# W_G of blocks 0 and 1 a block later, between W_A and W_B, by seven half-size products in turn, with its normalized rows kept in DRAM

## The chip, the cores and the metric

One Trainium2 chip; the program runs on one of its cores. The metric is the device time of one execution in microseconds, lower is better. A core has a matrix engine (PE, with its weight loads shown as PEld), a vector engine (DVE), a scalar engine (ACT), GpSimd (POOL), a synchronisation engine (SP), and 16 DMA engines that all queues share. In this kernel weights are asked for on SP's queue (q1 in the profile) and activations mostly on POOL's (q0).

## What is computed

One encoder layer over 2048 prompt tokens and 64 sample tokens, all matrices 1024 wide, fp32. Cut to what matters here:

```python
h = rms_norm(x, g_pre)
vA, bA, cA, zA, q, f, iv, zB, gA, gB = split_cols(h @ w_in)
yA = (silu(zA) * bA * causal_conv3(cA * vA)) @ w_a_out             # W_A
yB = (o * silu(zB)) @ w_b_out                                      # W_B, o from the HGRN2 scan
merged = sigmoid(gA) * yA + sigmoid(gB) * yB
x = x + rms_norm(merged @ w_o, g_post)                             # W_O
gate = sigmoid(rms_norm(x, g_ple) @ w_ple_gate)                    # W_G
x = x + (p @ w_ple_proj) * gate
```

The last two lines are the subject: `h2 = rms_norm(x, g_ple)` is multiplied by the gate matrix W_G, and the output is `x + p*gate`, where `p` stands here for the projected `p @ w_ple_proj`.

## The kernel before

The 2112 tokens are three blocks of 704 columns (BN), each two halves of 352 (HN). Activations are feature-major: eight tiles of 128 x 704, one for each 128 features, in a ring of 52 tiles (tag `r`), plus nine half-wide ones (`hf`). Every fp32 product is three matmuls: weights and activations are split into a rounded high part and a low rest (`split`: one ACT copy, one DVE subtraction), and hi*hi, hi*lo and lo*hi are added up in PSUM (five banks `pg` for these products). A matmul takes one 128 x 128 weight and 352 columns.

A weight tile is 128 x 512 fp32, 256 KB: half of one 128-wide column of a matrix. `load_raw` asks SP for it (five buffers `raw`), ACT makes `hi` (four buffers), and the low part is either made by DVE or, when it was stored in DRAM earlier (`lows`), loaded by SP into one of seven buffers (`lo`, four, and `s`, three).

Large products go three ways:

- plain (`gemm`, lines 530 to 539): 16 weight tiles and 384 matmuls for a 1024 x 1024 matrix and one block. Each weight tile (with its low part) serves 24 matmuls.
- Strassen-Winograd by column pair (`sgroup`, lines 343 to 386): seven products of half size in place of eight, all seven at once.
- the same seven products in turn (`in_turn`, lines 464 to 517): product n = 0 to 6 over all four column pairs g, then the next n. 336 matmuls for a matrix and block; each weight tile serves 12 matmuls, since each of the seven products has its own combined weight (`A11, A12, S2, S3, A22, S1, S4`; the S tiles are sums made once and stored in DRAM, by `prepare_sums`, lines 303 to 341). The activations' combinations are made by DVE and ACT one product ahead (`operand_of`, lines 452 to 462, called by `prepare`). After product 1, 4, 5 and 6 of a pair a `sink` takes a finished half tile. A generator yields after each product, and the caller then issues the loads for what follows.

The order of a block: attention path (`path_b`), convolution path (`path_a`), W_A, W_B (together `merge` in block 0, in turn in blocks 1 and 2), W_O (in turn in block 2 only, else plain, `final_out`), then seven groups of the next block's gates (`run(fills, LEAD)`, line 1381), under which `final_norm` makes the new `x` and `h2` a step at a time, then W_G (`final_gate`, line 1383), and the next block's path_b. In blocks 0 and 1, `final_norm` spills `x` to DRAM, splits `h2` into hi and lo tiles, and `final_gate` does eight plain `gemm`s, reloads `x` and `p`, applies the sigmoid and stores `y_fm`. The third block's W_G is done at the end of the program, half by half.

Queues are served in order: a DMA that POOL issues waits for its operand, and those behind it wait too. Reloads marked `pace=True` wait for the last matmul traced so far (line 242). Instructions within an engine stand in the order that the tile scheduler gave them at build time, and ring tiles are handed out in the order of the program.

The sums of W_A and W_B are prepared in block 0 under `merge`; those of W_O under block 1's `path_a`, one column pair for each of its last four steps j (`side`, lines 1331 to 1337).

Of the kernel before, what the change touches and what calls it, by code (L numbers as in the profile page):

```python
# [82 lines left out]
def hybrid_step(  # L83
# [219 lines left out]
    def prepare_sums(firsts, ahead):  # L303
# [23 lines left out]
        for n, (i1, _) in enumerate(groups):  # L327
            a11, a21, a22, a12 = nxt
            if ahead and n + 1 < len(groups):
                nxt = load(*groups[n + 1])  # L330
            V.tensor_tensor(a22, a21, a22, ALU.add)
            keep("S1", i1, a22)
            V.tensor_tensor(a21, a11, a21, ALU.subtract)
            keep("S3", i1, a21)
            V.tensor_tensor(a11, a22, a11, ALU.subtract)
            keep("S2", i1, a11)
            V.tensor_tensor(a12, a12, a11, ALU.subtract)
            keep("S4", i1, a12)
            if not ahead and n + 1 < len(groups):
                nxt = load(*groups[n + 1])  # L340
            yield
# [740 lines left out]
    def merge_in_turn(a, kept, mg, made):  # L1082
# [31 lines left out]
        ], loads  # L1114

# [25 lines left out]
    def final_norm(bl, segs, xo, acc, h2, kept):  # L1141
# [26 lines left out]
        for j in range(KB):  # L1168
            xj = xo[j][:, c]
            if kept is not None:  # L1170
                kept["x", j] = spill("x", j)
                G.dma_start(kept["x", j], xo[j])
            if len(h2) <= j:
# [6 lines left out]
    def final_gate(bl, segs, xo, h2, kept, anew=False):  # L1180
        c = slice(segs[0]["off"], segs[-1]["off"] + HN)
        for j in range(KB):
            if not bl["last"]:
                pss = gemm(W_G + j, h2, segs)
            elif j == 0:
# [4 lines left out]
            xj = reload(kept["x", j]) if ("x", j) in kept else xo[j]  # L1190
            pj = kept["p", j] if bl["last"] else reload(kept["p", j])
# [5 lines left out]
            (SP if bl["last"] and j >= KB - 2 else G).dma_start(y_fm[j * P : (j + 1) * P, segs[0]["t0"] : segs[0]["t0"] + len(segs) * HN], t[:, c])  # L1197
# [122 lines left out]
    for bi, bl in enumerate(blocks):  # L1320
# [8 lines left out]
        sums_ahead = prepare_sums((W_A, W_B), True) if first else prepare_sums((W_O,), False) if bi == 1 else iter(())  # L1329
# [19 lines left out]
        else:  # L1349
# [22 lines left out]
        if nxt:  # L1372
# [10 lines left out]
            run(final_gate(bl, segs, xo, h2, kept))  # L1383
        else:
            gate = [final_gate(bl, [s], xo, h2, kept, anew=s is segs[1]) for s in segs]
# [54 lines left out]
```

## Time and profile before

| | |
|---|---|
| device time, median of 3 runs | 2664.5 us (2657.28, 2667.55, 2664.5) |
| span of the profiled execution | 2661.4 us, 3.1 us under that median; its page gives no time outside the span |
| busy: PE, PEld, DVE, ACT, POOL | 99%, 98%, 65%, 54%, 13% of the span |
| moved by DMA | 735.00 MB, mean 276 GB/s |
| W_G of block 0, of block 1 | 969.4 to 1031.0 us, 1825.1 to 1886.8 us |
| W_A and W_B in turn, block 1 | 1545 to 1655 us |
| W_A, W_B, W_O in turn, block 2 | 2400 to 2565 us |

The matrix engine hardly ever waits. A matmul of 352 columns is shown as some 324 ns long, but matmuls overlap, so that the distance from one to the next, about 160 ns, is what counts: a stretch's length divided by its matmuls. In the windows view each row gives a stretch, its length, the busy time and (in brackets) the number of instructions of each engine, the granted PE clock, the share of time that the 16 DMA engines were busy, and GB/s.

### The profile page before, as it was taken

How to read it: one execution, taken by the hardware profiler on the slowest of the kernel's cores; microseconds unless marked ns; L12 is line 12 of the kernel's file. 1: busy time of each engine (PE TensorE's matmuls, PEld its weight loads, DVE VectorE, ACT ScalarE, POOL GpSimd, SP SyncE). 2: the span in 40 equal slices, each digit the busy share in tenths (PEclk: the TensorE clock that was granted, in tenths of full speed). 3: DMA queues.
4: the chain of work that ended last, by engine and by line, in shares of the span. 5: the costliest groups of instructions: out<-in, count | busy, mean ns of one | idle time of the engine just before them, and what ended most of it. 6: DMA issues, size and time to landing. Idle time of an engine off the chain costs nothing.

```text
span 2661.4 us, 47775 instructions
## 1 busy us (share of the span) xinstructions
PE 2623.0 (99%) x16748; PEld 2600.4 (98%) x16748; DVE 1727.0 (65%) x3341; ACT 1449.6 (54%) x2782; POOL 349.1 (13%) x649
## 2 busy tenths in 40 slices
PE   7999999999999999999999999999999999999998
PEld 7999999999999999999999999999999999999988
DVE  7788888998667545466645578443355564447857
ACT  5655655454334544566645565454566654445664
POOL 1000000100432210001112210021000000001011
PEclk9999999999999999999999999999999999999999
DMA  8677777898998988776789988599867678889975
GB/s 304 217 263 269 244 260 271 299 316 288 367 344 285 352 289 275 252 227 221 222 287 357 391 304 306 182 352 307 276 218 222 222 224 263 273 274 319 302 234 168
DMA packets 362097, 735.00 MB, mean 276 GB/s; under 512 B 44064, under 2 KB 48704, under 8 KB 361856
## 3 DMA queue, kind: packets, MB, share of 16 engines
q1 hardware_dynamic: 324864, 588.20, 65.9%
q0 software_dynamic: 36704, 143.70, 14.9%
q8 instruction: 132, 2.16, 0.3%
q14 instruction: 109, 0.89, 0.1%
q10 hardware_dynamic: 288, 0.05, 0.0%
HBM read 525.71 MB, written 206.06 MB: 275 GB/s over the span
## 4 chain that ended last, share of the span: by engine, by line
PE 88%; DMA 4%; issue 3%; DVE 3%; ACT 1%; POOL 1%; SPq 0%; DVEq 0%; ACTq 0%; POOLq 0%
PE pg L357 19%; PE pg L358 19%; PE pg L359 19%; PE pg L523 4%; PE pg L525 4%; PE pg L524 4%; PE pg L491 3%; PE pg L490 3%; PE pg L492 3%; PE pa L957 1%; PE pa L921 1%; PE pa L911 1%; PE pa L959 1%; PE pa L910 1%; DMA low<-s 1%
## 5 line engine op out<-in xcount | busy, mean ns | idle before, releaser
L357 PE MATMUL pg<-r,hi 128*128 128x352 f32 x3304 | 1095.0, 332 | 6.8 <-DVE r L403 2.7
L358 PE MATMUL pg<-r,hi 128*128 128x352 f32 x3304 | 1070.1, 324 | 0.0
L359 PE MATMUL pg<-r,lo 128*128 128x352 f32 x2356 | 763.6, 324 | 0.0
L214 ACT CAST hi<-raw 128x512 fp32r<-128x512 f32 x708 | 435.6, 619 | 573.1 <-PE pg L358 206.5
L357 PEld LDWEIGHTS pg<-r,hi 128*128 128x128 f32 x3304 | 624.3, 189 | 12.6 <-DVE r L865 4.6
L358 PEld LDWEIGHTS pg<-r,hi 128*128 128x128 f32 x3304 | 623.9, 189 | 0.0
L359 PEld LDWEIGHTS pg<-r,lo 128*128 128x128 f32 x2356 | 443.9, 188 | 0.0
L359 PE MATMUL pg<-r,s 128*128 128x352 f32 x948 | 306.9, 324 | 0.0
L523 PE MATMUL pg<-r,hi 128*128 128x352 f32 x896 | 289.4, 325 | 3.1 <-ACT r L1194 2.1
L524 PE MATMUL pg<-r,hi 128*128 128x352 f32 x896 | 289.8, 324 | 0.6 <-DVE r L184 0.6
L525 PE MATMUL pg<-r,lo 128*128 128x352 f32 x756 | 244.6, 324 | 0.4 <-DVE lo L184 0.2
L184 ACT CAST hi<-raw 128x512 fp32r<-128x512 f32 x234 | 143.4, 619 | 165.4 <-PE pg L358 48.3
L184 DVE TENSOR_TENSOR r<-r,r 128x352 fp32r<-128x352 f32 (+3 forms) x274 | 169.9, 638 | 60.7 <-ACT r L184 60.0
L184 DVE TENSOR_TENSOR lo<-raw,hi 128x512 fp32r<-128x512 f32 x234 | 159.6, 688 | 65.8 <-ACT hi L184 54.2
L184 ACT CAST r<-r 128x352 fp32r<-128x352 f32 (+3 forms) x274 | 150.4, 578 | 75.1 <-DVE r L666 18.2
L184 ACT CAST hi<-s 128x512 fp32r<-128x512 f32 x160 | 99.1, 619 | 154.8 <-PE pg L358 132.7
L491 PE MATMUL pg<-r,hi 128*128 128x352 f32 x560 | 181.8, 326 | 0.0
L359 PEld LDWEIGHTS pg<-r,s 128*128 128x128 f32 x948 | 178.9, 189 | 0.1
L490 PE MATMUL pg<-r,hi 128*128 128x352 f32 x560 | 178.4, 326 | 0.1
L523 PEld LDWEIGHTS pg<-r,hi 128*128 128x128 f32 x896 | 168.0, 188 | 5.5 <-ACT r L1194 2.4
L524 PEld LDWEIGHTS pg<-r,hi 128*128 128x128 f32 x896 | 168.6, 188 | 2.0 <-DVE r L184 1.7
L371 ACT COPY hf<-pg 128x352 f32<-128x352 f32 x354 | 156.0, 446 | 6.9 <-PE pg L359 6.3
(358 smaller groups left out, 4096.9 us busy)
## 6 DMA issues: line engine op xcount, KB each, us to landing
raw<-w_blk SPq DMA_DIRECT2D x590, 256.0 KB, 4.0
lo<-low SPq DMA_DIRECT2D x404, 256.0 KB, 3.9
raw<-S SPq DMA_DIRECT2D x392, 256.0 KB, 4.1
low<-lo SPq DMA_DIRECT2D x346, 256.0 KB, 3.8
s<-low SPq DMA_DIRECT2D x304, 256.0 KB, 3.9
S<-s SPq DMA_DIRECT2D x160, 256.0 KB, 3.3
r<-w_blk POOLq DMA_DIRECT2D x48, 256.0 KB, 7.3
S<-r POOLq DMA_DIRECT2D x48, 256.0 KB, 6.1
```

Source lines behind the costliest of these rows:

```text
L184: return A.copy(hi, src).ins, V.tensor_tensor(lo, src, hi.bitcast(F32), ALU.subtract).ins
L214: A.copy(hi, raw)
L357: add(hi[:, k, :], xhi, start=start and k == 0, stop=False)
L358: add(hi[:, k, :], xlo, start=False, stop=False)
L359: last[0] = add(lo[:, k, :], xhi, start=False, stop=k == KH - 1).ins
L371: copied = A.copy(got[n], ps[bank])
L490: add(hi[:, k, :], xhi, start=start and k == 0, stop=False)
L491: add(hi[:, k, :], xlo, start=False, stop=False)
L492: last[0] = add(lo[:, k, :], xhi, start=False, stop=k == KH - 1).ins
L523: T.matmul(ps, hi[:, k % 4, :], xhi[:, c], start=k == ks[0], stop=False)
L524: T.matmul(ps, hi[:, k % 4, :], xlo[:, c], start=False, stop=False)
L525: last[0] = T.matmul(ps, lo[:, k % 4, :], xhi[:, c], start=False, stop=k == ks[-1]).ins
```

## The change

W_G of block b (b = 0, 1) is no longer done at the end of block b. Its `h2` rows, not split, are written to DRAM by `final_norm`. In block b + 1 a new stage stands between W_A and W_B in the list that `in_turn` works through: seven products in turn on W_G, with `h2`, `x` and `p` loaded from DRAM on POOL's queue, and a sink that applies the sigmoid and stores `y_fm` in half tiles. The loads of the `o` rows and of the first `GB` gates, which W_B needs, move from W_A's products 3, 5 and 6 to W_G's. For the seven products W_G needs sums: `prepare_sums` makes them under block 1's `path_a`, with the low parts of three plain tiles for each pair as well, and W_O's sums move to block 2's `path_a`. The third block's W_G stays plain at the end; it takes stored low parts where there are any, and splits the other tiles anew.

```diff
-                parts.append(split_w(raw, None if anew else (idx, half_)))
+                parts.append(split_w(raw, None if anew or (idx >= W_G and (idx, half_) not in lows) else (idx, half_)))
...
-    def prepare_sums(firsts, ahead):
+    def prepare_sums(firsts, ahead, plain=False):
...
             a11, a21, a22, a12 = nxt
+            for t, key in ((a11, (i1, 0)), (a12, (i1, 1)), (a22, (i1 + KH, 1))) if plain else ():
+                lows[key] = dram.tile([P, 4, P], F32, tag=f"lo{key}", name=nm("low"), bufs=1)
+                lo = tile_of(F32R)
+                split(t, lo, lo)
+                G.dma_start(lows[key], lo.bitcast(F32))
...
-                (W_A, 3): ("o", ob),
-                (W_A, 5): ("o", ob),
-                (W_A, 6): (GB, mg),
+                (W_G, 3): ("o", ob),
+                (W_G, 5): ("o", ob),
+                (W_G, 6): (GB, mg),
                 (W_B, 1): (GB, mg),
...
+    def gate_in_turn(bl, kept):
+        h2, xp = [], {}
+        def fetch(j, h, pair):
+            for kind, t in zip("xp", pair):
+                G.dma_start(t, kept[kind, j][:, h * HN : (h + 1) * HN])
+            xp[j, h] = pair
+        def loads(idx, n):
+            if (idx, n) in ((W_A, 3), (W_A, 5)):
+                h2.extend(reload(kept["h2", j], True) for j in range(len(h2), len(h2) + KH))
+            if (idx, n) in ((W_A, 6), (W_G, 4)):
+                for j in range(0, KH, 2):
+                    both = rt(), rt()
+                    for q in range(2):
+                        fetch(j + q, int(idx == W_G), [half(t, q) for t in both])
+            if (idx, n) == (W_G, 1):
+                for j in range(KH, KB):
+                    both = rt(), rt()
+                    for h in range(2):
+                        fetch(j, h, [half(t, h) for t in both])
+        def sink(g, c, h, x, y):
+            j = g + c * KH
+            v = whole(x, y)
+            gate = hf() if y is None else v
+            A.activation(gate, v, AF.Sigmoid)
+            xt, pt = xp.pop((j, h))
+            V.tensor_tensor(pt, pt, gate, ALU.mult)
+            V.tensor_tensor(pt, pt, xt, ALU.add)
+            o = bl["t0"] + h * HN
+            G.dma_start(y_fm[j * P : (j + 1) * P, o : o + HN], pt)
+        return dict(idx=W_G, raw=h2, sink=sink, anew=()), loads
...
             V.scalar_tensor_tensor(t[:, c], xj, g_ple[:, j : j + 1], rs2[:, c], ALU.mult, ALU.mult)
-            split(t[:, c], h2[j][0][:, c], h2[j][1][:, c])
+            if kept is not None:
+                kept["h2", j] = spill("h2", j)
+                G.dma_start(kept["h2", j], t)
+            else:
+                split(t[:, c], h2[j][0][:, c], h2[j][1][:, c])
...
-        sums_ahead = prepare_sums((W_A, W_B), True) if first else prepare_sums((W_O,), False) if bi == 1 else iter(())
+        sums_ahead = prepare_sums((W_A, W_B), True) if first else prepare_sums((W_G,) if bi == 1 else (W_O,), False, bi == 1)
...
             stages, loads = merge_in_turn(a, kept, mg, made)
+            gate, gate_loads = gate_in_turn(blocks[bi - 1], kepts[bi - 1])
+            stages.insert(1, gate)
...
             for idx, n in in_turn(stages, a_first):
                 loads(idx, n)
+                gate_loads(idx, n)
...
-            run(final_gate(bl, segs, xo, h2, kept))
```

More of the change, by code (lines that the diff above doesn't have):

```diff
@@ L1176, in final_norm, with final_gate @@
             V.scalar_tensor_tensor(t[:, c], xj, g_ple[:, j : j + 1], rs2[:, c], ALU.mult, ALU.mult)
[L1177 removed]
+            if kept is not None:
[3 more added lines that the diff above has]
+                split(t[:, c], h2[j][0][:, c], h2[j][1][:, c])
             yield
[L1180 removed]
+    def final_gate(bl, segs, xo, h2, kept, anew):
         c = slice(segs[0]["off"], segs[-1]["off"] + HN)
         for j in range(KB):
[L1183 to L1185 removed]
+            if j == 0:
                 both = gemm_by_k([W_G, W_G + 1], h2, segs, anew)
@@ L1189, in final_gate @@
                 pss = both[1] if j == 1 else gemm(W_G + j, h2, segs, anew)
-            xj = reload(kept["x", j]) if ("x", j) in kept else xo[j]
-            pj = kept["p", j] if bl["last"] else reload(kept["p", j])
+            xj, pj = xo[j], kept["p", j]
             t = rt()
@@ L1196, in final_gate @@
             V.tensor_tensor(t[:, c], t[:, c], xj[:, c], ALU.add)
-            (SP if bl["last"] and j >= KB - 2 else G).dma_start(y_fm[j * P : (j + 1) * P, segs[0]["t0"] : segs[0]["t0"] + len(segs) * HN], t[:, c])
+            (SP if j >= KB - 2 else G).dma_start(y_fm[j * P : (j + 1) * P, segs[0]["t0"] : segs[0]["t0"] + len(segs) * HN], t[:, c])
             yield
@@ L1382, in hybrid_step @@
             assert not hooks
-            run(final_gate(bl, segs, xo, h2, kept))
         else:
-            gate = [final_gate(bl, [s], xo, h2, kept, anew=s is segs[1]) for s in segs]
+            gate = [final_gate(bl, [s], xo, h2, kept, s is segs[1]) for s in segs]
             spread_out((norms[0], (2, 1, 0, 0, 1, 1, 4, 4)), (norms[1], (0,) * 6 + (1, 1) + (2, 2, 2, 2, 1, 0, 1, 3, 3, 2)))
```

2 lines of the change are left out of this document (1 added, 1 removed).

## The prediction

> **What bounds the kernel now.** I read the page's head first, then the stretches of the stages that the change touches, then the DMA issues.
>
> ```profile
> span 2661.4 us, 47775 instructions
> PE 2623.0 (99%) x16748; PEld 2600.4 (98%) x16748; DVE 1727.0 (65%) x3341; ACT 1449.6 (54%) x2782; POOL 349.1 (13%) x649
> PEclk9999999999999999999999999999999999999999
> ```
>
> The matrix engine is busy 99% of the span, with a granted clock of nine tenths or more in every slice. What it is given to do sets the time, as long as its operands come. So the change is worth its matmuls, less the waits that it makes. The pitch of the matmuls comes from the windows view (length, PE busy with its count, granted clock, DMA share, GB/s): first W_G of blocks 0 and 1.
>
> ```profile
> 969.40:1031.00 61.60, 61.60 (x386) 1.00 0.85 284
> 1825.10:1886.80 61.70, 61.70 (x386) 1.00 0.82 277
> ```
>
> (61.60 + 61.70) / 772 = 159.7 ns a matmul. The same view with all engines (PE, PEld, DVE, ACT, POOL) shows 110 us of block 1's path_a, under which W_O's sums are made; then the stages in turn, block 1's W_A and W_B and block 2's W_A, W_B and W_O; and the last W_G.
>
> ```profile
> 1420.00:1530.00 110.00, 110.00 (x685) 109.97 (x684) 64.41 (x124) 60.16 (x122) 27.98 (x62) 1.00 1.04 388
> ...
> 1545.00:1599.50 54.50, 54.50 (x339) 54.27 (x338) 39.05 (x81) 32.88 (x70) 6.35 (x12) 1.00 0.88 303
> 1599.50:1655.00 55.50, 55.40 (x337) 53.91 (x336) 45.82 (x101) 34.92 (x75) 5.32 (x11) 1.00 0.89 304
> ...
> 2400.00:2455.00 55.00, 55.00 (x342) 54.72 (x341) 39.49 (x82) 33.51 (x70) 6.63 (x13) 1.00 0.90 314
> 2455.00:2510.00 55.00, 55.00 (x340) 54.57 (x339) 49.51 (x107) 33.41 (x70) 5.02 (x10) 1.00 0.94 316
> 2510.00:2565.20 55.20, 55.20 (x343) 54.05 (x342) 34.68 (x77) 37.08 (x82) 5.22 (x9) 1.00 0.79 252
> 2588.00:2656.50 68.50, 65.20 (x397) 62.75 (x395) 50.11 (x101) 33.15 (x68) 10.79 (x19) 1.00 0.58 193
> ```
>
> In turn, the five stages give 275.2 us / 1701 = 161.8 ns, seams between stages included. The reader is to see the last two columns: in turn W_A and W_B already keep the DMA engines busy 0.88 to 0.94 of their time, where plain W_G needed 0.82 to 0.85. In the first row, at 388 GB/s and a share of 1.04, they are full. Over those 110 us PE lost nothing (110.00 / 685 = 160.6 ns), so full DMA engines alone cost nothing while the weights get their part.
>
> **The change part by part.**
>
> *Matmuls.* Two plain W_G go: 2 x 384 x 159.7 ns = 122.6 us. Two in turn come: 2 x 336 x 161.8 ns = 108.7 us. **Saved: 13.8 us** (6.9 a block). Nothing else in the change can make the kernel faster, so this is the most it can bring.
>
> *Weights.* For the bytes, the page's DMA issues and the DMA view's list (KB each, median us to landing):
>
> ```profile
> raw<-w_blk SPq DMA_DIRECT2D x590, 256.0 KB, 4.0
> lo<-low SPq DMA_DIRECT2D x404, 256.0 KB, 3.9
> ...
> r<-o POOLq DMA_DIRECT2D x24, 352.0 KB, 6.6
> ...
> r<-x_fm POOLq DMA_DIRECT2D x16, 176.0 KB, 4.7
> ```
>
> A weight tile is 0.262 MB, a ring tile 0.360 MB, a half tile 0.180 MB. One product in turn is 48 matmuls, by the first stage's pitch (54.50 / 339) 7.72 us; it needs four weight tiles and four low parts, 2.10 MB, since none of W_G's products is split anew. At 0.388 MB/us a product's time carries 3.00 MB, so **0.90 MB a product are left for POOL's queue**. In the plain form the same 2.10 MB served 96 matmuls.
>
> *Activations on POOL's queue.* In before W_A and W_B ask for four tiles (1.44 MB) after W_A's 1, 3, 5, 6 and W_B's 1. Now W_A's 3 and 5 bring `h2` (1.44 MB each), W_A's 6 eight halves of x and p (1.44), W_G's 1 sixteen halves (2.88), W_G's 3 `o` (1.44), 4 eight halves (1.44), 5 `o` (1.44), and the sinks of products 1, 4, 5, 6 store 0.72 MB of `y_fm` each. What POOL's queue is behind, product by product, 0.90 MB carried off in each: W_A4 0.54, W_A5 0, W_A6 0.54, W_G0 1.08, W_G1 0.90, W_G2 2.88, W_G3 1.98, W_G4 3.24, W_G5 4.50, W_G6 5.76 MB. The last 0.72 MB of output nobody waits for; **5.04 MB are left, 13.0 us at 0.388 MB/us**. W_B's first operands (`o`) and the halves for W_G's last sink are part of it, so the matrix engine can't pass W_G without them.
>
> Against it stand the weights asked for ahead: five `raw` and seven low buffers. Twelve tiles are 3.1 MB; I count eight, 2.1 MB, as time lent, since the last four must be there when a product begins. W_B's first two products need only half the weights and pay it back. Then (5.04 - 2.1) / 0.388 = 7.6 us a block. Bounds: 13.0 if nothing is lent, 0 if the buffers and W_B's light start take it all. I take **7.6 us, 15.1 us for both blocks**, nearer the middle because in before each 1.44 MB burst was absorbed without a wait, but never two in a row without a product between.
>
> How the queues share shows in 1595 to 1599 us, such a burst, when `o` tiles are fetched (queue, kind: packets, MB, share of 16 engines):
>
> ```profile
> q0 software_dynamic: 277, 1.22, 77.2%
> q1 hardware_dynamic: 187, 0.35, 23.0%
> ```
>
> POOL's queue took 77% of the engines' time and the weights 23%. So a backlog shows as weights that come late, less as late activations. The Trainium skill says under "DMA: Bandwidth & Descriptors", section "Queues, rings and completion order", that each DMA engine takes the queues in turn, a packet at a time; these rows agree, with 1.22 / 277 = 4.4 KB a packet against 0.35 / 187 = 1.9 KB. By equal shares of bytes the activations would be late instead of the weights; the sum is the same.
>
> *Vector and scalar engine in the new stage.* From the groups:
>
> ```profile
> L1087 DVE TENSOR_TENSOR r<-hf,r 128x352 f32<-128x352 f32 x48 | 24.9, 521 | 0.6
> L1194 ACT ACTIVATE r<-pg 128x352 f32<-128x352 f32 x48 | 21.7, 460 | 52.4 <-PE pg L525 52.4
> L1043 POOL DMA_DIRECT2D r<-x x16 | 8.6, 538 | 7.8 <-DVE r L184 5.3 <-issue 2.5
> ```
>
> For a column pair DVE has 24 half-wide operations over the seven products (seven operands narrowed, four more for T2, two sums, three in `whole`, eight in the sinks): 24 x 4 x 521 ns = 50 us of 54. Block 2's W_B above has 49.51 of 55.00 with PE busy 55.00, so this is taken as hidden by PE. ACT gets 16 sigmoids of 460 ns beside its copies, 7.4 us on some 33 of 55. POOL issues about 60 DMAs of 538 ns, 32 us of 54. Cost 0; if the cover were gone, the seam pays DVE's surplus of product 5 (five operations, 2.6 us a pair against 1.93), 2.7 us a block.
>
> *`h2` to DRAM.* The stretches of the two blocks in which `final_norm` spills `x`:
>
> ```profile
> 931.00:969.40 38.40, 38.40 (x242) 38.40 (x242) 22.18 (x33) 24.09 (x44) 3.31 (x6) 0.99 0.91 303
> 1785.00:1825.20 40.20, 40.20 (x247) 40.20 (x247) 20.62 (x30) 24.08 (x44) 3.31 (x6) 0.96 0.87 303
> ```
>
> Now 16 stores of 0.360 MB come in place of 16 splits. They fall into 38.4 and 40.2 us at 303 GB/s; 2.88 MB more there are 75 GB/s, together 378, under 388. Cost 0, covered by the gates' matmuls; without that cover 2.88 / 0.388 = 7.4 us a block. Path_b now follows the fills at once.
>
> *Sums.* W_O's move to block 2, into a stretch like the row 1420 to 1530, which cost PE nothing. W_G's, in their old place, store twelve more tiles, 3.1 MB or 8.1 us of full DMA; twelve more splits lie on engines that are busy 64 and 60 of 110 us. POOL's loads and the GA reloads behind them come later. The stretch before W_A has no room left, W_A's first two products (raw weights only) have 1.05 MB each, of which the first comes in time for the reloads. Bounds 0 and (3.1 - 1.05) / 0.388 = 5.3 us; I take 1.0, as W_A needs no low parts at its start.
>
> *The end.* The last W_G splits four tiles anew whose low parts it loaded before:
>
> ```profile
> L184 DVE TENSOR_TENSOR lo<-raw,hi 128x512 fp32r<-128x512 f32 x234 | 159.6, 688 | 65.8 <-ACT hi L184 54.2
> ```
>
> Four such operations are 2.8 us at most, where PE idles 3.3 of 68.50 us. I take 0.5.
>
> **Sum:** -13.8 + 15.1 + 1.0 + 0.5 = +2.8 us on the span, 2664.2. The median of the runs lies 3.1 us above it: **2667 us**, no change that can be told (I call 0.5%, 13.3 us, what this kernel's runs can tell; they spread by 10.3 us).
>
> **The rivals.**
>
> *All transfers are hidden.* The buffers and W_B's light start absorb everything: -13.8 + 0.5 gives 2651. For it: PE ran at full pitch through 110 us of full DMA engines, and no burst of before made it wait. Against it: there the demand just fitted, here W_G alone asks for 14.7 MB of weights and 10.1 MB on POOL's queue (sixteen and eight halves, eight `o` tiles, sixteen half outputs) in 54.4 us, over 450 GB/s.
>
> *Late halves stop the vector engine.* DVE works in order. If a half tile of p isn't there when its gate is, the multiplication waits, and behind it stand the operands of the next product, for which PE waits. It decides from W_G's product 6 on: its eight halves are asked for one product, 7.7 us, ahead, behind `o` and output stores that are themselves late. Then nothing is lent, since weights in hand don't help: 13.0 us a block, and the sums' 5.3 as the same wait in path_a: -13.8 + 26.0 + 5.3 + 0.5 = +18, 2682, slower. For it: DVE has 4 us of spare time in 54 to catch up. Against it: POOL's 77% share.
>
> *The change doesn't do what it says*: the scheduler sets loads or sinks at other places in the queues, so that `o` isn't there at W_B. The ring holds (at most 48 of 52 tiles by the code in W_G's product 5: m 8, h2 8, operands 8, mid 4, halves 12, o 8). One reload that waits a whole product more costs 7.7 us a block: 2682.
>
> *A lower ceiling.* "DMA: Bandwidth & Descriptors", section "Specifications" of the Trainium skill, gives some 358 GB/s from HBM for one core. By it 0.66 MB a product are left, the backlog is 7.08 MB, (7.08 - 2.1) / 0.358 = 13.9 us a block, 2680. The row at 388 GB/s over 110 us speaks against it; the measurement decides.
>
> **How the numbers follow.** Forecast 0.50 (its own range 2655 to 2678), hidden 0.17, late halves 0.28, wrong order 0.03, lower ceiling 0.02. Faster than 2651.2: two thirds of the hidden case and a little of the forecast, 0.13. Slower than 2677.8: most of the last three and a tenth of the forecast, 0.31. The range is 2650 (saving alone, all else 0) to 2688 (nothing lent, 26.0, sums 5.3, end 2.8, and one block's DVE surplus of 2.7: 2664.5 - 13.8 + 36.8 = 2687.5).
>
> **What would show it.** 96 matmuls fewer (16652). Right: a W_G stretch between W_A and W_B near 390 GB/s with share about 1.0 and some 62 us long, PE's waits in its second half released by ACT's `hi` or by DMAs of low parts. Hidden: 54 to 55 us. Late halves: DVE waits on DMAs of `x` and `p`. Elsewhere, gates followed at once by path_b, without a gap. Wrong altogether if W_G's stage runs at full DMA rate and full pitch, or if PE waits in path_a by more than 5 us.

## The result and the profile after

The changed kernel takes **2694.9 us** (median of 4 runs, 2692.63 to 2699.03) against 2664.6 us (2657.28 to 2667.55) for the kernel before on the same chip: ratio **1.0115, 95% interval 1.0095 to 1.0135**, some 30 us slower. The prediction, 2667 us with a range of 2650 to 2688, was wrong: it said no change that can be told.

The page of the changed kernel: its span, the busy times, and the chain that ended last.

```profile
span 2697.3 us, 48294 instructions
PE 2624.8 (97%) x16652; PEld 2593.2 (96%) x16652; DVE 1789.5 (66%) x3517; ACT 1500.0 (56%) x2898; POOL 426.6 (16%) x789
...
PE 80%; DMA 10%; DVE 3%; issue 3%; ACT 2%; POOL 1%; SPq 0%; DVEq 0%; ACTq 0%; POOLq 0%
```

And the chain of the kernel before, the same line of its page.

```profile
PE 88%; DMA 4%; issue 3%; DVE 3%; ACT 1%; POOL 1%; SPq 0%; DVEq 0%; ACTq 0%; POOLq 0%
```

The 96 matmuls are gone (16748 to 16652), but PE is busy for as long as before, 2624.8 us against 2623.0, in a span 35.9 us longer. The share of DMA in the chain went from 4% to 10%. (The profiled execution of the changed kernel was its slowest, 2699.03 us, so the spans differ by more than the medians.)

Stage by stage, the windows view of the changed kernel (start and end, length, busy time and instructions of PE, PEld, DVE, ACT, POOL, granted PE clock, DMA share, GB/s): block 1's gates and path_b in one, its path_a, W_A, W_G and W_B; then block 2's W_A, W_G and W_B, and the end.

```profile
866.00:1266.30 400.30, 393.71 (x2597) 390.99 (x2596) 222.60 (x469) 240.56 (x443) 49.72 (x83) 0.99 0.77 264
1266.30:1495.80 229.50, 226.12 (x1422) 224.54 (x1421) 128.44 (x261) 125.30 (x257) 55.30 (x119) 1.00 0.95 342
1495.80:1553.20 57.40, 55.05 (x339) 54.19 (x338) 41.92 (x87) 33.09 (x70) 9.15 (x18) 1.00 0.87 305
1553.20:1618.80 65.60, 59.60 (x337) 57.67 (x335) 38.82 (x85) 35.86 (x78) 24.74 (x47) 0.92 1.00 362
1618.80:1681.20 62.40, 57.67 (x337) 55.68 (x337) 51.13 (x113) 38.02 (x82) 7.92 (x16) 0.97 0.88 305
2362.10:2416.40 54.30, 54.30 (x337) 54.04 (x337) 38.74 (x81) 33.02 (x69) 9.03 (x17) 1.00 0.88 308
2416.40:2480.10 63.70, 56.95 (x339) 53.96 (x337) 38.67 (x86) 36.10 (x78) 25.00 (x47) 1.00 1.01 372
2480.10:2540.00 59.90, 55.65 (x337) 54.22 (x338) 54.14 (x119) 36.42 (x77) 7.78 (x15) 1.00 0.95 333
2596.40:2697.30 100.90, 88.26 (x518) 84.61 (x516) 66.63 (x136) 47.94 (x103) 14.12 (x23) 0.95 0.52 166
```

The same stretches of the kernel before, as far as they are not shown above (gates, path_b, path_a, W_B of block 1, the end).

```profile
864.80:969.30 104.50, 102.32 (x637) 101.30 (x636) 57.84 (x88) 63.42 (x118) 17.52 (x30) 0.98 0.94 334
1031.10:1320.20 289.10, 289.10 (x1961) 288.15 (x1961) 171.66 (x387) 181.50 (x332) 28.34 (x46) 1.00 0.72 233
1320.20:1545.00 224.80, 224.80 (x1422) 224.65 (x1421) 123.60 (x255) 118.43 (x245) 49.11 (x107) 1.00 0.95 338
1599.40:1655.00 55.60, 55.50 (x337) 54.01 (x337) 45.92 (x101) 34.95 (x75) 5.32 (x11) 1.00 0.89 304
2565.30:2661.40 96.10, 84.42 (x518) 80.95 (x516) 64.02 (x132) 47.60 (x103) 14.08 (x23) 0.99 0.57 185
```

The reader is to see W_G at a DMA share of 1.00 and 1.01, W_B behind it slower although its DMA share is as before, and block 1's path_a, W_A and gates slower with no product of W_G in them. All stretches, from first matmul to first matmul, in us:

| | before | after | difference |
|---|---|---|---|
| W_G of blocks 0 and 1 | 61.8 + 61.9 | 65.6 + 63.7 | +5.6 |
| W_B in turn, blocks 1 and 2 | 55.6 + 54.6 | 62.4 + 59.9 | +12.1 |
| path_a and W_A, block 1 | 224.8 + 54.4 | 229.5 + 57.4 | +7.7 |
| path_a and W_A, block 2 | 278.6 | 279.1 | +0.5 |
| gates and path_b, block 1 | 104.5 + 289.1 | 400.3 | +6.7 |
| gates and path_b, block 2 | 394.8 | 391.9 | -2.9 |
| W_O, and all ahead of 866 us | 985.2 | 986.6 | +1.4 |
| the end | 96.1 | 100.9 | +4.8 |
| span | 2661.4 | 2697.3 | +35.9 |

What W_G moves by DMA, in its stage of block 1 (queue, kind: packets, MB, share of 16 engines), and what the weight loads of PE wait for there (us in total, times, longest):

```profile
q1 hardware_dynamic: 7647, 13.90, 59.8%
q0 software_dynamic: 3170, 9.76, 40.3%
```

```profile
PEld pg L497 <- DMA s<-low: 3.9, 1, 3.9
PEld pg L495 <- ACT r L184: 3.1, 3, 1.3
```

One wait is a low part that came late. The others, for the high part of an operand, come from late weights too: the timeline of ACT shows the cast of a weight waiting for its DMA, and the operand's cast (L184) two places behind it.

```profile
1561.06 0.62 ACT L214 CAST hi<-raw 128x512 fp32r<-128x512 f32 x1 [2.57 <-DMA raw<-w_blk]
1561.59 0.45 ACT L501 COPY r<-pg 128x352 f32<-128x352 f32 x1
1561.93 0.49 ACT L184 CAST r<-r 128x352 fp32r<-128x352 f32 x1
```

In W_B the waits are mostly on DVE and on casts of operands; one, of 1.5 us, is on a low part:

```profile
PEld pg L496 <- DVE r L184: 2.6, 3, 1.6
PEld pg L495 <- ACT r L184: 2.2, 2, 1.9
PEld pg L497 <- DMA lo<-low: 1.5, 1, 1.5
```

ACT makes these casts, and in W_B of block 1 it waits for DVE above all (L1100 is in W_B's own sink). Neither ACT nor DVE waits there for a DMA of an activation, in block 1 or in block 2.

```profile
ACT r L184 <- DVE r L1100: 7.6, 7, 2.6
```

In block 1's path_a (two rows) PE's weight loads wait for late low parts alone, in W_A behind it (one row) for DVE alone:

```profile
PEld pg L364 <- DMA s<-low: 2.6, 2, 1.6
PEld pg L364 <- DMA lo<-low: 2.2, 3, 1.0
PEld pg L496 <- DVE r L184: 3.2, 3, 1.4
```

### The profile page after: what moved, and what is told of

The parts are those of the page before. It is cut to its first block, busy times and chain, and to the rows that moved or that the text cites. A ratio compares the mean times of both kernels' runs of the same rounds, so it can differ in the third digit from the quotient of the medians.

```text
span 2697.3 us, 48294 instructions
## 1 busy us (share of the span) xinstructions
PE 2624.8 (97%) x16652; PEld 2593.2 (96%) x16652; DVE 1789.5 (66%) x3517; ACT 1500.0 (56%) x2898; POOL 426.6 (16%) x789
## 4 chain that ended last, share of the span: by engine, by line
PE 80%; DMA 10%; DVE 3%; issue 3%; ACT 2%; POOL 1%; SPq 0%; DVEq 0%; ACTq 0%; POOLq 0%
PE pg L362 18%; PE pg L364 17%; PE pg L363 17%; PE pg L495 3%; PE pg L496 3%; PE pg L497 3%; PE pg L528 3%; PE pg L530 3%; PE pg L529 3%; DMA raw<-S 3%; DMA raw<-w_blk 2%; DMA s<-low 2%; DMA lo<-low 1%; PE pa L962 1%; PE pa L926 1%
## 5 line engine op out<-in xcount | busy, mean ns | idle before, releaser
L214 ACT CAST hi<-raw 128x512 fp32r<-128x512 f32 x744 | 458.9, 621 | 607.6 <-PE pg L363 197.0
L364 PE MATMUL pg<-r,lo 128*128 128x352 f32 x2356 | 763.3, 324 | 4.0 <-DMA lo<-low 4.0
L362 PEld LDWEIGHTS pg<-r,hi 128*128 128x128 f32 x3304 | 622.9, 189 | 13.7 <-issue 4.8
L363 PEld LDWEIGHTS pg<-r,hi 128*128 128x128 f32 x3304 | 622.7, 188 | 0.0
L184 DVE TENSOR_TENSOR r<-r,r 128x352 fp32r<-128x352 f32 (+3 forms) x334 | 197.1, 613 | 58.7 <-ACT r L184 57.8
L184 ACT CAST r<-r 128x352 fp32r<-128x352 f32 (+3 forms) x334 | 175.4, 560 | 77.2 <-DVE r L671 17.9
L184 ACT CAST hi<-raw 128x512 fp32r<-128x512 f32 x222 | 136.1, 620 | 139.2 <-PE pg L363 37.4
L184 ACT CAST hi<-s 128x512 fp32r<-128x512 f32 x160 | 99.3, 621 | 153.7 <-PE pg L363 140.1
L530 PE MATMUL pg<-r,lo 128*128 128x352 f32 x564 | 183.4, 325 | 0.3 <-DVE lo L184 0.2
L184 DVE TENSOR_TENSOR lo<-raw,hi 128x512 fp32r<-128x512 f32 x222 | 151.4, 688 | 44.1 <-ACT hi L184 32.4
L497 PE MATMUL pg<-r,lo 128*128 128x352 f32 x504 | 164.6, 327 | 4.5 <-DMA lo<-low 4.5
L495 PEld LDWEIGHTS pg<-r,hi 128*128 128x128 f32 x784 | 147.6, 191 | 12.6 <-ACT r L184 11.1
```

The lines of the kernel that those rows point to most:

```text
L184: return A.copy(hi, src).ins, V.tensor_tensor(lo, src, hi.bitcast(F32), ALU.subtract).ins
L214: A.copy(hi, raw)
L362: add(hi[:, k, :], xhi, start=start and k == 0, stop=False)
L363: add(hi[:, k, :], xlo, start=False, stop=False)
L364: last[0] = add(lo[:, k, :], xhi, start=False, stop=k == KH - 1).ins
L495: add(hi[:, k, :], xhi, start=start and k == 0, stop=False)
```

## The experiments

Sixteen kernels. Lengths in us from the windows view; "gates + b" and "path_a" are block 1's; two lengths are those of blocks 1 and 2; the ratio is to the kernel before on the same chip.

| kernel | median | ratio, interval | gates + b | path_a | W_A | W_G | W_B | end |
|---|---|---|---|---|---|---|---|---|
| before | 2664.6 | 1 | 393.6 | 224.8 | 54.4, 54.4 | | 55.6, 54.6 | 96.1 |
| after | 2694.9 | 1.0115, 1.0095-1.0135 | 400.3 | 229.5 | 57.4, 54.3 | 65.6, 63.7 | 62.4, 59.9 | 100.9 |
| e1_no_xp | 2684.2 | 1.0074, 1.0049-1.0100 | 398.3 | 229.1 | 59.0, 54.4 | 57.9, 57.6 | 60.6, 59.5 | 101.5 |
| e2_no_low_parts | 2678.2 | 1.0053, 1.0038-1.0068 | 397.4 | 229.0 | 58.2, 54.4 | 56.0, 56.2 | 58.6, 57.3 | 100.5 |
| e3_no_add | 2689.9 | 1.0094, 1.0077-1.0112 | 394.9 | 229.2 | 57.5, 54.4 | 63.7, 61.7 | 58.8, 57.6 | 100.3 |
| e4_early | 2688.4 | 1.0093, 1.0078-1.0108 | 398.5 | 232.0 | 59.4, 56.0 | 59.2, 59.2 | 59.9, 58.4 | 100.9 |
| e5_full_lows | 2691.3 | 1.0102, 1.0080-1.0123 | 400.8 | 232.7 | 56.8, 54.4 | 65.6, 62.7 | 63.9, 61.2 | 98.1 |
| e6_no_spill | 2690.9 | 1.0100, 1.0083-1.0117 | 392.5 | 230.4 | 56.9, 54.3 | 63.7, 61.9 | 62.0, 61.2 | 101.1 |
| e7_no_low_store | 2691.8 | 1.0103, 1.0087-1.0119 | 399.4 | 224.9 | 54.5, 54.4 | 62.8, 62.3 | 62.5, 59.6 | 104.0 |
| e8_sums_spread | 2699.5 | 1.0135, 1.0118-1.0152 | 396.5 | 233.3 | 54.4, 54.3 | 61.8, 63.3 | 62.7, 61.6 | 100.7 |
| e9_no_low_no_xp | 2681.1 | 1.0069, 1.0051-1.0087 | 401.0 | 229.1 | 59.1, 54.3 | 56.3, 56.2 | 60.1, 57.8 | 100.7 |
| e10_no_low_no_add | 2669.1 | 1.0023, 1.0010-1.0037 | 400.1 | 230.2 | 57.5, 54.4 | 55.8, 55.9 | 55.7, 54.6 | 101.4 |
| e11_early_anew | 2685.9 | 1.0082, 1.0063-1.0100 | 397.8 | 224.9 | 59.8, 55.5 | 63.5, 58.7 | 61.4, 57.7 | 99.0 |
| e12_recompute | 2671.9 | 1.0035, 1.0021-1.0049 | 391.8 | 225.8 | 57.1, 55.3 | 59.0, 59.4 | 59.8, 57.8 | 98.0 |
| e13_pool_add | 2681.0 | 1.0064, 1.0049-1.0079 | 393.5 | 224.8 | 56.0, 55.1 | 63.9, 62.4 | 60.3, 58.8 | 99.7 |
| e14_pool_add_s2 | 2677.8 | 1.0046, 1.0029-1.0062 | 395.4 | 224.8 | 56.0, 55.3 | 59.6, 59.4 | 60.2, 58.6 | 100.1 |
| e15_recompute_no_add | 2665.4 | 1.0016, 1.0003-1.0028 | 395.5 | 226.1 | 56.0, 55.1 | 60.6, 57.5 | 56.8, 55.2 | 98.0 |
| e16_recompute_s2 | 2672.6 | 1.0038, 1.0024-1.0052 | 394.3 | 224.8 | 54.9, 55.4 | 57.7, 56.6 | 60.2, 57.7 | 100.0 |

### W_G's stage: weights, halves or the vector engine

```diff
 # e1_no_xp: nothing loaded, another tile in place of x and p
-            xt, pt = xp.pop((j, h))
-            V.tensor_tensor(pt, pt, gate, ALU.mult)
-            V.tensor_tensor(pt, pt, xt, ALU.add)
+            pt = rt(HN)
+            V.tensor_tensor(pt, keep[:, :HN], gate, ALU.mult)
+            V.tensor_tensor(pt, pt, keep[:, :HN], ALU.add)
 # e2_no_low_parts, in split_w, for W_G's stage
+        if only_hi[0]:
+            A.copy(hi, raw)
+            return hi, hi
 # e3_no_add
-            V.tensor_tensor(pt, pt, xt, ALU.add)
 # e4_early: o one product earlier; h2 from ahead of W_A on, x and p whole, in W_A's products
-                (W_G, 3): ("o", ob),
-                (W_G, 5): ("o", ob),
+                (W_G, 2): ("o", ob),
+                (W_G, 4): ("o", ob),
...
+            if (idx, n) in ((W_A, -1), (W_A, 0)):
+                h2.extend(reload(kept["h2", j], n >= 0) for j in range(len(h2), len(h2) + KH))
+            for j in {(W_A, 2): (0, 1), (W_A, 3): (2, 3), (W_A, 5): (4, 5), (W_A, 6): (6, 7)}.get((idx, n), ()):
+                xp[j] = [reload(kept[kind, j], True) for kind in "xp"]
```

> Leaves out: the 64 half-tile loads of x and p (11.5 MB over both blocks); the sinks do the same operations on a constant tile, so y_fm is not x + p*gate. Theory D (DMA time: W_G's stage asks for more than the 16 engines move, weights land late, the ACT queue stands behind them): without x and p POOL's backlog at W_G's end is 2.34 MB, under the 2.1 MB lent and the last outputs, so nearly all of the 35 us of waits in the stages in turn go: 2662 to 2670 us. Theory V (the vector engine's surplus in the sinks and operands makes operands late): the same operations are there, 2688 to 2697 us. Theory O (o and GB come late only because they stand behind output stores in POOL's queue): W_B's waits of some 8 us a block stay, 2678 to 2685.

> Leaves out: the low parts of W_G's weights in turn; the high part is used in their place, so the gates are less exact. 14.7 MB fewer over both blocks on SP's queue, the same matmuls and the same loads on POOL's. D: weights then need 1.05 MB a product, 1.95 MB are left for POOL, its largest backlog is about 1 MB: the waits go, 2662 to 2670 us. V: 2688 to 2697. O: the order on POOL's queue is as before, W_B's waits stay, 2675 to 2685.

> Leaves out: the addition of x in W_G's sinks in turn, 16 half-wide DVE operations a block (8.3 us of DVE a block); x is still loaded, y_fm is p*gate there. D: no change beyond 4 us, 2690 to 2697 us. V: the vector engine gets 8.3 us of slack in each W_G, waits fall by 8 to 16 us, 2679 to 2687. O: as D.

> The same computation; only loads are moved: h2 before and after W_A's product 0, x and p as whole tiles after W_A's 2, 3, 5 and 6 (16 loads a block instead of 32), o after W_G's 2 and 4. W_A's first two products need only half the weight bytes, so they have 1.95 MB each to spare that the changed kernel leaves unused. D: from W_A's product 0 to W_G's end 42.4 MB are asked for and 42.0 MB can be moved, so waits in the stages in turn fall from 35 us to 0 to 10: 2662 to 2675 us. V: no change, 2688 to 2697. O: o is ahead of the late outputs, W_B's waits go, W_G's stay: 2678 to 2687.

Windows of the kernel without low parts: W_G and W_B of block 1.

```profile
1551.40:1607.40 56.00, 54.74 (x337) 53.88 (x337) 40.67 (x90) 38.06 (x82) 24.86 (x47) 1.00 0.90 316
1607.40:1666.00 58.60, 56.08 (x339) 53.99 (x338) 48.59 (x108) 35.75 (x78) 6.96 (x13) 1.00 0.88 308
```

W_G's stage is bound by bytes for the most part. 28 low parts fewer (7.3 MB) bring it from 65.6 and 63.7 to 56.0 and 56.2 us, with the DMA share down to 0.90; 32 halves fewer (5.8 MB) bring 57.9 and 57.6. Leaving out the addition wins only 2 us there. Asked for earlier (e4), the same bytes cost less in W_G, but W_A then takes 2.0 and 1.7 us more. What none of the four explains is W_B, which stays 2.7 to 5.0 us longer than before. The times of e1, e2 and e4 lie 8 to 14 us above theory D's ranges. Those of e1 and e2 lie in theory O's, but O doesn't hold: in W_B neither ACT nor DVE waits for a DMA of `o` or of the gates (above), and in e10 below, with POOL's queue in the same order, W_B takes as long as before.

### Stores of h2, stores of low parts, the end

```diff
 # e5_full_lows: the fourth plain tile's low part is stored as well
-            for t, key in ((a11, (i1, 0)), (a12, (i1, 1)), (a22, (i1 + KH, 1))) if plain else ():
+            for t, key in ((a11, (i1, 0)), (a12, (i1, 1)), (a21, (i1 + KH, 0)), (a22, (i1 + KH, 1))) if plain else ():
 # e6_no_spill: x is loaded in h2's place
-                kept["h2", j] = spill("h2", j)
-                G.dma_start(kept["h2", j], t)
+                pass
 # e7_no_low_store: W_G's plain tiles load another tile's low part
-        ... prepare_sums((W_G,) if bi == 1 else (W_O,), False, bi == 1)
+        ... prepare_sums((W_G,) if bi == 1 else (W_O,), False)
 # e8_sums_spread
-                if j >= 3:
+                if j in ((0, 1, 2, 4, 6) if bi == 1 else (3, 4, 5, 6, 7)):
                     next(sums_, None)
```

> The same computation; the low part of the fourth plain tile of each W_G pair is stored too (four stores and four splits more under block 1's path_a), so that the last W_G loads all its low parts for its first half, as in before. If the four DVE splits at the end are what lengthens it: from the last in-turn matmul to the end 96.2 us as in before instead of 101.0, and path_a 1 to 2 us longer; 2690 to 2694 us. If the end is longer for another reason (the order of the instructions there): 101 us, 2695 to 2698.

> Leaves out: the 16 stores of h2 (5.8 MB); W_G in turn reads x in its place, so the gates of blocks 0 and 1 are wrong. If the stores cost time (they fill the DMA engines while block 1's fills run and squeeze the weights): fills and path_b of block 1 fall from 400.2 us to the 393.6 of before; 2687 to 2691 us. If that loss comes from the cover that W_G at the end of block 0 gave (path_b begins while the vector engine still works off final_norm): no change, 2693 to 2697.

> Leaves out: the twelve plain low parts that the sums' preparation makes and stores for W_G under block 1's path_a (3.1 MB); W_G in turn loads another stored low part in their place (as many bytes, wrong values), and the last W_G splits all its tiles anew, which may lengthen the end by itself. If these stores are the loss there: block 1's path_a 229.5 to 225 us and its W_A 57.3 to 54.4, 7 us together. If the loss is the sums' place in the order: both unchanged.

> The same computation; W_G's sums are prepared over steps 0, 1, 2, 4 and 6 of block 1's path_a instead of its last five, one pair in two steps, and end before W_A. D (DMA time): path_a carries 389 GB/s already with W_O's sums, so the twelve stores more had no room; spread out they have it: path_a 225 us, W_A 54.4 us, 2686 to 2690 us. Rival (vector and scalar engine work of the twelve splits): path_a as long as before, 2693 to 2697.

The kernel that doesn't store `h2`, gates and path_b of block 1:

```profile
862.70:965.20 102.50, 100.77 (x637) 99.77 (x637) 51.72 (x82) 58.26 (x110) 16.43 (x28) 1.00 0.93 332
965.20:1255.20 290.00, 289.40 (x1963) 288.18 (x1962) 171.24 (x388) 182.17 (x333) 28.87 (x47) 1.00 0.73 237
```

The kernel that neither makes nor stores W_G's plain low parts, path_a and W_A of block 1:

```profile
1267.10:1492.00 224.90, 224.90 (x1422) 224.66 (x1421) 123.68 (x255) 118.63 (x245) 49.09 (x107) 1.00 0.95 338
1492.00:1546.50 54.50, 54.50 (x338) 54.16 (x337) 38.82 (x81) 32.85 (x69) 8.46 (x16) 1.00 0.89 310
```

Without the twelve low parts PE is busy for the whole of path_a and W_A again: 279.4 us against 286.9, so nearly all of the 7.7 us there are their doing (the median hardly shows it: this kernel splits sixteen tiles anew at the end, 104.0 us). 4.7 us of it are lost in path_a, where PE waits only for low parts that land late, so there it is DMA time; 3.0 in W_A, where PE waits only for DVE, which has 41.92 us of work there against 39.05 in the row of the kernel before. Whether the twelve splits or path_a's late weights push that work over the seam, no run tells apart. Spread over earlier steps (e8) the low parts free W_A, but path_a is 3.8 us longer still, again with PE waiting for nothing but low parts (8.7 us), and the time, 2699.5, lies above both forecasts; there is no room in path_a for 3.1 MB. Without the `h2` stores the gates and path_b take 392.5 us, 7.8 less; PE's weight loads, which wait there for low parts for 3.2 us in the changed kernel, wait for none. A single kernel can mislead here: the eleven kernels with these stores lie between 394.9 and 401.0 us (mean 398.6), the seven without between 391.8 and 395.5 (393.8), so that they cost about 4.8 us. In block 2 the same two groups do not differ (means 393.4 and 393.2).

The end stays open. With all low parts stored it takes 98.1 us (e5), with four tiles split anew 100.3 to 101.5, with sixteen 104.0; but the kernels from e11 on split eight and take 98.0 to 100.1. The number of tiles doesn't order it, and no experiment took its other causes apart.

### What slows W_B

e9 joins the edits of e1 and e2, e10 those of e2 and e3.

> Leaves out: the low parts of W_G's weights in turn (the high part stands in) and the loads of x and p (a constant tile stands in): 26 MB fewer, the same operations on every engine. If all waits of W_G and of W_B behind it are DMA time: W_G 54 to 55 us and W_B 55 to 56 in both blocks, 2660 to 2667 us. If W_B waits for operands because the vector engine works off W_G's sinks: W_G 54 to 56, W_B still 58 to 60, 2668 to 2675.

> Leaves out: the low parts of W_G's weights in turn and the addition of x in its sinks. If W_B's loss is the vector engine's lag: W_B 55.5 to 57 us in both blocks, W_G 55 to 56, 2668 to 2673 us. If it is DMA time alone: W_B as with the low parts alone left out, 58.6 and 57.4 us, 2675 to 2680.

Windows of e9, W_G and W_B of block 1:

```profile
1553.00:1609.30 56.30, 55.05 (x339) 53.97 (x337) 40.10 (x89) 37.26 (x81) 10.76 (x20) 1.00 0.67 213
1609.30:1669.40 60.10, 55.99 (x337) 54.06 (x338) 49.76 (x111) 36.26 (x79) 8.06 (x16) 1.00 0.88 302
```

Windows of e10, the same two stages:

```profile
1550.80:1606.60 55.80, 54.66 (x338) 53.84 (x336) 37.12 (x80) 38.51 (x83) 25.12 (x47) 1.00 0.92 321
1606.60:1662.30 55.70, 55.29 (x338) 53.80 (x337) 46.25 (x102) 35.12 (x77) 6.41 (x12) 1.00 0.91 317
```

e9 takes nearly all pressure off the DMA engines in W_G (share 0.67) and W_B still needs 60.1 and 57.8 us. Its time, 2681.1, lies above both of its forecasts. e10 leaves the pressure (0.92) and takes 16 vector operations a stage out beside the low parts, and W_B is back at 55.7 and 54.6 us, its time before. The DVE column says how: 51.13 us of vector work stand in W_B of block 1 after the change, 49.76 in e9, 46.25 in e10, 45.92 before. W_G's last sinks are done late, in W_B, ahead of the operands that its products wait for. The last of them in the changed kernel, an addition, starts 11.4 us after W_B's first matmul:

```profile
1630.24 0.52 DVE L1153 TENSOR_TENSOR r<-r,r 128x352 f32<-128x352 f32 x1
```

But e10 leaves out two things, and each has its part. The addition is worth 3.6 and 2.3 us of W_B (the changed kernel against e3), or 2.9 and 2.7 where the low parts are out (e2 against e10). The low parts are worth 3.8 and 2.6 (the changed kernel against e2), or 3.1 and 3.0 where the addition is out (e3 against e10). So about half of W_B's loss is DVE's own work in the sinks, and about half goes with W_G's low parts: without them DVE waits less in W_G for ACT's casts of operands, which stand behind those of late weights (4.2 us in e2, 6.4 in the changed kernel), and less of its work is left over for W_B (48.59 us in e2). Leaving out the loads of x and p as well (e9) does not help W_B; why it is longer there than in e2 is open.

### Fewer bytes, all computed

```diff
 # e11_early_anew: e4, and A11 and S3 of W_G split anew, their low parts neither stored nor loaded
+    fresh = ("A11", "S3")
...
-        return dict(idx=W_G, raw=h2, sink=sink, anew=()), loads
+        return dict(idx=W_G, raw=h2, sink=sink, anew=fresh), loads
 # e12_recompute: as e11, and h2 made from x and one tile of rs2 in W_A's products, not stored
+                V.scalar_tensor_tensor(t, xt8[j], g_ple[:, j : j + 1], rs[0], ALU.mult, ALU.mult)
 # e13_pool_add: as e12
-            V.tensor_tensor(pt, pt, xt, ALU.add)
+            G.tensor_tensor(pt, pt, xt, ALU.add)
 # e14_pool_add_s2: as e13; e16_recompute_s2: as e12
-    fresh = ("A11", "S3")
+    fresh = ("A11", "S2", "S3")
 # e15_recompute_no_add: as e12
-            V.tensor_tensor(pt, pt, xt, ALU.add)
```

> The same computation: loads early as in e4, and W_G's products on A11 and S3, in which the vector engine has time, split their weights anew; their low parts are neither stored under path_a nor loaded (4.2 MB fewer loads, 2.1 MB fewer stores). D: W_G 56 to 58 us, path_a and W_A of block 1 together 4 us shorter than changed, the end 1 to 2 longer (eight tiles split anew instead of four): 2677 to 2684 us. V: W_G longer than in e4, since DVE gets 5.5 us more work: 2688 to 2693.

> The same computation: as e11, and h2 is made again in block b + 1 from the x tiles that the sinks need anyway and one stored tile of row factors, so that h2 is neither stored nor loaded (11.5 MB fewer); DVE gets 6.1 us more in each W_A. D: fills and path_b of block 1 fall by the 5.8 us that the stores took, W_G to 55 to 57 us: 2666 to 2674 us, near before. V: W_A and W_G grow by the vector engine's 6 us, 2684 to 2692.

> The kernel of e12, but the addition of x in the sinks of W_G's stage is done by GpSimd in place of the vector engine; nothing is left out. If what is left of the loss in and behind W_G's stage is the vector engine's work (8 additions of a column pair, 32 in a stage, some 17 us of its 54): W_B goes from 59.8 and 57.8 us in e12 towards 55.7 and 54.6 (e10, without low parts and addition), W_G's stage loses one or two us, and the time falls by 5 to 10 us, to 2662 to 2667 us. Rival: the rest of the loss is late weights (low parts) and the half clock behind each such wait: then W_B and W_G stay within 1 us and the time within 2670 to 2674 us. Second rival: GpSimd's additions hold up the loads and stores that it issues in the same order, or slow the vector engine: the time rises above 2674 us, with waits of PE on operands of W_G's products 5 and 6 or of W_B.

> As e13, and the sums S2 of W_G are split anew as well, so that 4 low parts fewer (1.05 MB) are loaded in a stage, for 4 more subtractions of 688 ns on the vector engine (2.8 us a stage). If late weights still cost time in e13, W_G's stage is shorter by up to 2 us a block and the time 1 to 4 us under e13. If the vector engine is what limits it, the four subtractions come on top and the time is 0 to 5 us above e13.

> The kernel of e12 with the addition of x left out of the sinks of W_G's stage (the stored output is p*gate for blocks 0 and 1): 32 vector operations of 521 ns fewer in a stage, 16.7 us, and nothing else changed; all loads stay. If the rest of the loss in and behind W_G's stage is the vector engine's work: W_B goes from 59.8 and 57.8 us in e12 to 54.5 to 56.5, W_G's stage from 59.1 and 59.4 to 56 to 58 (one wait for a low part stays), and the time to 2658 to 2664 us. Rival: it is late weights: W_B stays above 57.5 in both blocks and the time within 2669 to 2674 us.

> The kernel of e12 with the sums S2 of W_G split anew; GpSimd does no addition; nothing is left out. 1.05 MB fewer are loaded in W_G's stage, the wait for a low part in its product 4 (2.3 us in e12, with 3.4 us at half clock) goes, and the vector engine has four subtractions of 688 ns more (2.8 us a stage). If late low parts are most of what W_G's stage still loses: it goes from 59.1 and 59.4 to 55 to 57 us and the time to 2664 to 2669 us. If the vector engine is the limit: W_G's stage stays above 58 or W_B grows by what it loses, and the time is 2670 to 2675 us.

e11's time, 2685.9, lies between its two forecasts: path_a came back to 224.9 us, but W_G of block 1 took 63.5 us, 4.8 of them in waits for low parts. e12 is the fastest kernel that does the moved W_G in full (e16 can't be told from it): 2671.9 us, 23 us under the changed kernel, and still 0.35% over the one before. That is in the range forecast for DMA time, though W_G came to 59 us and not to 55 to 57. Its W_G and W_B of block 1:

```profile
1541.10:1600.10 59.00, 56.74 (x337) 55.49 (x337) 44.51 (x95) 37.25 (x81) 13.41 (x25) 0.97 0.94 327
1600.10:1659.90 59.80, 56.13 (x339) 53.98 (x337) 50.18 (x112) 36.46 (x78) 8.23 (x16) 1.00 0.87 295
```

Without the addition (e15), W_B of block 1:

```profile
1602.40:1659.20 56.80, 55.56 (x338) 53.93 (x337) 47.44 (x105) 35.96 (x77) 7.48 (x15) 1.00 0.88 305
```

Vector work alone was taken away, and W_B got 3.0 and 2.6 us shorter: that part of its loss is the vector engine's, with the DMA relieved too. (The forecasts of e13 and e15 count 32 additions in a stage; the code makes 16, 8.3 us.) Fewer low parts (e16) bring W_G from 59.0 and 59.4 to 57.7 and 56.6 and leave W_B where it was; the median does not show it. Both causes hold: the bytes in W_G, and both together in W_B. What was expected of e15 in W_G did not come in block 1, which took 60.6 us with 3.4 in waits for low parts; block 2's took 57.5, and the median, 2665.4, lies above its forecast. Even this kernel, with work left out, is not faster than the one before. e13's second rival came true, in a way that the last section shows. e14's W_G takes 59.6 and 59.4 us, e13's 63.9 and 62.4, as forecast for late weights; the intervals of their times overlap.

## Why the prediction was wrong

**Matmuls, -13.8: right.** 96 went, and where nothing waits a stage in turn takes 54.3 us (block 2's W_A). 2 x 54.4 against 123.7 us is -14.9.

**DMA in W_G, +15.1: the right mechanism, too small.** Full DMA engines, waits on casts and low parts, in the places named. Measured: 65.6 + 63.7 - 108.8 = 20.5 us. The 11.2 and 9.3 us a block lie between the 7.6 taken and the 13.0 with nothing lent. Which part of the sum was off isn't taken apart; the record shows two things. 13.90 + 9.76 = 23.7 MB pass in the 65.6 us, at 362 GB/s and in block 2 at 372, not 388. And with 26 MB fewer over both blocks (e9) the stage still takes 56.3 and 56.2 us, so that 1.8 or 1.9 us a block are not bytes. The share also came out otherwise: over the stage POOL's queue had 40% of the engines, not the 77% of a single burst.

**Vector engine, "Cost 0": the step that failed.** I compared DVE's 50 us with PE's 54 in W_G alone, found it hidden, and priced the loss of that cover at 2.7 us a block. Two stages in a row were loaded, W_G and W_B with 46 and 49 us of its own, so a lag at the seam had nowhere to be made good. W_B lost 6.8 and 5.3 us, 12.1 in all where the sum had nothing: the largest of its errors. The addition in the sinks is 3.6 and 2.3 us of it (e3; 3.0 and 2.6 between e12 and e15); with the low parts left out as well (e10) all of it is gone. So the lag also grows with the weights that come late in W_G: the sum had the DMA and the vector engine as two terms that do not touch. The quote of W_B with 49.51 us of 55.00 was a row against me: it showed a stage without slack, and I read it as proof of cover.

**`h2` to DRAM, "Cost 0, covered by the gates' matmuls": failed.** Some 4.8 us in block 1 (by the two groups of kernels; e6 alone gives 7.8); the price without cover, 7.4, was the nearer. Adding up a mean rate, 303 + 75 = 378 GB/s, hid that the stores come between gates that load weights at a share of 0.94. In block 2 no loss is seen (-2.9 in these two profiles, 0.2 between the groups).

**Sums, +1.0: mis-sized, and beyond its bound of 5.3.** 7.7 us, nearly all of it the making and storing of the twelve low parts (e7). 4.7 of them are lost in path_a itself, in waits for low parts, a stretch that I had taken as free because its full DMA engines "cost nothing"; at a share of 1.04 and 388 GB/s it had no room for 3.1 MB more. The other 3.0 are waits on DVE in W_A. My reason for 1.0, that W_A needs no low parts at its start, passed over DVE, which W_A does need. W_O's sums in block 2 cost 0.5, as forecast.

**End, +0.5:** 4.8 in the profile; 2.8 between e5 and the changed kernel, the cause of the rest not found.

**All ends together:** with nothing covered my own prices give -13.8 + 26.0 + 5.3 + 2.8 + 14.8 + 5.4 = +40.5; the span grew by 35.9. That this is near is partly luck: the terms are off both ways (20.5 us measured for 26.0, 12.1 for 5.4, 4.8 for 14.8). The range, up to +23, left out both stores of `h2` and half of DVE's surplus, as if each term could go wrong alone.

**Clock: no term.** See below; up to some 11 us of the losses above, by an estimate there, are waits paid again at half speed.

**The rivals.** The halves of x and p did not stop DVE: its waits in W_G of block 1 are all on PE and ACT, none on a DMA, so the slower outcome came about in another way than that rival said, although its 2682 us was as near as any. The lower ceiling isn't one either: 388 GB/s was held in path_a, 372 over W_G in block 2. Transfers hidden: refuted by e1 and e2. Another order in the queues: not seen, since nothing in W_B waited for `o`.

## What to carry to other kernels

A form that saves an eighth of the matmuls and uses each weight tile half as often is worth only what the DMA engines have free in that stage; count its bytes against the rate there, and add the stores that prepare it, wherever they fall. "Hidden by PE" has to hold over two neighbouring stages, for each in-order engine: a stage filled to 90% hides its own work but no lag from the one ahead. Where a kernel has no slack anywhere, take the priced-if-uncovered ends of several small terms together, since they fall together.

## What the runs showed of the hardware

**A wait can be paid again at half clock.** Windows of 3.4 us of the changed kernel in W_G and W_B: one at full work, then pairs of a stretch with waits and the one behind it, and two stretches with waits (1578.10, and 2462.20 in W_G of block 2) that had no such sequel.

```profile
1557.70:1561.10 3.40, 3.40 (x23) 3.40 (x23) 0.92 (x2) 0.83 (x4) 0.00 (x0) 1.00 1.03 376
1561.10:1564.50 3.40, 1.99 (x10) 1.17 (x8) 0.59 (x2) 2.67 (x6) 0.00 (x0) 1.00 1.05 385
1564.50:1567.90 3.40, 3.40 (x12) 3.40 (x13) 1.70 (x4) 1.36 (x3) 0.00 (x0) 0.50 1.01 368
1578.10:1581.50 3.40, 2.42 (x16) 2.13 (x14) 1.16 (x3) 1.77 (x4) 2.35 (x5) 1.00 0.86 241
1588.40:1591.80 3.40, 1.31 (x9) 1.02 (x7) 0.00 (x0) 1.61 (x4) 2.16 (x5) 1.00 1.05 378
1591.80:1595.20 3.40, 1.88 (x6) 1.88 (x7) 0.00 (x0) 0.00 (x0) 0.51 (x1) 0.50 1.04 387
2462.20:2465.60 3.40, 1.72 (x11) 1.43 (x10) 1.05 (x2) 1.02 (x2) 1.80 (x5) 1.00 1.04 376
```

12 matmuls instead of 23 in the stretch from 1564.5 us, with no wait in it: the granted clock is 0.50. It went down behind stretches in which PE was busy for 1.99 and 1.31 us of 3.4, not behind 2.42, and not behind 1.72 in block 2, whose W_G lost 6.75 us of PE time at a clock of 1.00 throughout. So PE's busy time in a stretch doesn't decide alone near 2 us, and what else does stays open. Cut at the period of these drops, the traces of all eighteen kernels, behind their first 100 us, have 46 stretches at full clock with less than 1.58 us of PE, and half clock follows every one; of 133 with 1.6 to 2.2 us it follows 22. By the records of the granted clock the changed kernel has 30.7 us of it after its first 100 us, the kernel before 10.2 (and one record more that runs out past its end); at (23 - 12) x 0.16 = 1.8 us for each 3.4, six more such stretches are an estimated 11 us at most. The Trainium skill ("TensorE: Matmul & The Clock Gate", "What's actually happening") has a free-running window of 3413 ns and half rate after an idle one. The period agrees: the drops at 1564.5, 1591.8 and 1622.5 us are 8 and 9 windows apart. But the window need not be idle; in the row from 1561.10 a busy share of 0.59 was little enough.

**GpSimd's additions stop the vector engine's.** In e13 the group of weight splits on DVE takes 879 ns where e12's takes 688, and DVE won nothing. The timeline of e13 (start, length):

```profile
1588.30 0.94 POOL L1150 TENSOR_TENSOR r<-r,r 128x352 f32<-128x352 f32 x1
...
1588.53 0.52 DVE L405 TENSOR_TENSOR hf<-r,pg 128x352 f32<-128x352 f32 x1 [0.33 <-PE pg L501]
...
1594.34 1.16 POOL L1150 TENSOR_TENSOR r<-r,r 128x352 f32<-128x352 f32 x1 [0.97 <-DVE r L1149]
1594.61 1.28 DVE L405 TENSOR_TENSOR hf<-r 128x352 f32<-128x352 f32 x1
```

An operation with one operand in PSUM (`pg`) runs beside GpSimd's in 0.52 us; the one with both in SBUF takes 1.28, to 0.39 us past the end of GpSimd's. The Trainium skill says so ("SBUF — State Buffer", "SBUF: two separate sides"): a vector operation with two SBUF inputs and a GpSimd operation that reads SBUF exclude each other, and the second waits for the whole of the first. These rows agree, as far as GpSimd's times can be trusted: 0.39 us past its end is less than the 0.52 of the operation alone.
